# A mixture of experts in pairs: tokens gathered for two pairs at a time from two rounded parts, and the scatter-back moved into the next pair's first product

## The chip, the cores and the metric

The program runs on one core of a Trainium2 chip. Its five engines run side by side and meet at semaphores: TensorE (PE in the profile; PEld is its weight load), VectorE (DVE), ScalarE (ACT), GpSimd (POOL) and SyncE (SP), which issues most of the DMAs. The metric is device time in microseconds (us), and lower is better. The kernel before took 2449.71 us, the median of 3 runs (2448.79 to 2453.85).

## The reference

`first_block` has two layers on 512 tokens of 1024 channels. Each layer is a mixer (a recurrent one, then a convolutional one) and after it a mixture of 16 experts. `second_block` then runs two more hybrid layers. The change touches the mixture alone, so it is what matters here:

```python
def _ec_moe(h, router, w1, w3, w2):
    cap = EC_CAPACITY * n // N_EXPERTS                      # 2 * 512 / 16 = 64 tokens an expert
    probs = softmax(h @ router, over the experts)
    gates, idx = lax.top_k(probs, cap)                      # every expert takes its 64 best tokens
    xs = h[bidx, idx]                                       # gather
    a = xs @ w1[e];  g = xs @ w3[e]                         # 1024 x 1024 each
    y = (silu(a) * g) @ w2[e] * gates                       # 1024 x 1024
    return zeros_like(h).at[bidx, idx].add(y)               # scatter back
```

`h` is `x` divided by its root mean square and multiplied and shifted per channel (`G` and `SH` in the kernel). All inputs are float32. Each layer reads 16 * 3 matrices of 4 MB, so 192 MB (192 loads of 1 MB) a layer.

## The kernel before

One `Builder` writes the whole program. A scheduler then sets the order on each engine from the dependencies and from its own estimate of times, so the order of the code is not the order on the engine.

`moe(l, fin)` handles the 16 experts of layer `l` in 8 pairs (`q`). The 64 tokens of one expert of a pair stand in rows 0 to 63, and those of the other in rows 64 to 127. The work of a pair is:

- **Gather** (L1104, `pick` at L1113): a matrix `oh` with a single 1 in each column, 512 tokens by 128 slots, picks the tokens. For each of 8 groups of channels, 4 float32 products of 128 columns (L1116) sum the tokens of `xn` (`x` times `rr`, made at L1093) into a PSUM bank. DVE (even groups, L1120) or ACT (odd groups, L1118) applies `G` and `SH` and writes `xs`.
- **Products** (`expert_mm`, L1132): `xs` is the stationary operand, 64 columns of it per expert, so that the two experts use the two halves of the array. For each 2 loads of weights (one per expert) there are 8 products of 512 columns, 4 for each half. w1, w3 and w2 take 32 products each (L1141; for w2 of the last pair L1239).
- **Gates** (L1122): 4 float32 products of 2 columns give every slot its probability.
- **Between w3 and w2**: ACT computes silu (L1196), DVE multiplies (L1197), PE transposes in two PSUM banks (L1205), and two copies follow (L1206).
- **Scatter** (`weigh` L1207, `scatter` L1213): DVE multiplies the result by the gates (L1209), ACT rounds it to float32r (L1210) and DVE takes the rest (L1211). For 4 blocks of tokens and 2 halves of the channels, 2 float32r products of 512 columns (L1217) with the matrix `sc` go to a bank `ac`, which DVE adds to `x` (L1218). `sc` comes from two small products with `eid` (L1190).

A float32 product is two instructions in the trace, each with its own weight load. A float32r product is one.

PSUM has 8 banks: 4 are called `mm`, 2 `tr` and 2 `ac`. The weights go through a ring of 1 MB tiles: 4 of the general ring, 1 of the persistent pool and `EXTRA` = 13 of their own, 18 in all. `EORDER` says in which order the ring takes them. SP loads a tile as soon as PE has finished with the one that stood there 18 loads earlier (L318). The first 18 loads go ahead of the first product.

The gather of a pair is written after the pair before it has done w3, and the scheduler draws part of it forward into w2 and into the next w1. The first pair (its tokens come from `rk`, a rank computed while routing) is gathered between its first products. Meanwhile DVE ranks all the experts (`topk`, L1144) for the later pairs.

Of the kernel before, what the change touches and what calls it, by code (L numbers as in the profile page):

```python
# [25 lines left out]
NT = 4  # L26
# [243 lines left out]
class Builder:  # L270
    NBASE = 4
    X1, X2, X3, X4, X5, X6 = 2, 1, 3, 1, 7, 1
    NSTREAM, SDEPTH, SBUFS = 3, 2, 4
    EXTRA = 13
    EORDER = ((3, 2, 8, 9, 10, 7, 11, 0, 1, -1, -1, -1, -1, 4, 5, 6, -2, 12), (-1, 7, 0, 6, 1, 8, 9, 10, -1, -1, 5, 11, -1, 2, 3, 4, -2, 12))

    def __init__(self, ctx, tc, a, out):
        self.ctx, self.tc, self.nc, self.a, self.out = ctx, tc, tc.nc, a, out
# [800 lines left out]
    def moe(self, l, fin):  # L1079

        nc, a, tc, x = self.nc, self.a, self.tc, self.x
        G, SH, pr, rr = self.G, self.SH, self.pr, self.rr
        self.rw.close()
        es = ExitStack()
        mp = es.enter_context(tc.tile_pool(name=f"M{l}", bufs=1, side="right", reuse_waits="tile"))
        pos = mp.tile([16, 512], BF16, name=f"pos{l}")
        pT = mp.tile([P, NT, 16], F32, name=f"pT{l}")
        gts = mp.tile([P, 8], F32, name=f"gts{l}")
        xn = self.pp.tile([P, NT, D], F32, tag="hp0", name=f"xn{l}")
        rt = self.pp.tile([P, KD // 2, 512], F32, tag="hp1", name=f"rt{l}")  # L1090
# [13 lines left out]
        def gather(q):  # L1104

            oh = mp.tile([P, NT, 2, 64], F32, tag="oh", name=self.nm("oh"))
            ps = pT[:, :, 2 * q:2 * q + 2] if q else self.rk
            self.oh = nc.vector.tensor_tensor(oh, self.iota[:, None, None, :].to_broadcast([P, NT, 2, 64]),  # L1108
                                    ps[:, :, :, None].to_broadcast([P, NT, 2, 64]), op=ALU.is_equal)
            xs = mp.tile([P, KD, P], F32, tag="xsT", name=self.nm("xsT"))  # L1110
            return xs, oh

        def pick(k, xs, oh):  # L1113
            p = self.mm("tr")[:, :P]
            for t in range(NT):
                nc.tensor.matmul(p, xn[:, t, k * P:(k + 1) * P], oh[:, t].rearrange("p e s -> p (e s)"), start=(t == 0), stop=(t == NT - 1))  # L1116
            if k % 2:
                nc.scalar.activation(out=xs[:, k], in_=p, func=AF.Identity, scale=G[:, k:k + 1], bias=SH[:, k:k + 1])  # L1118
            else:
                nc.vector.tensor_scalar(xs[:, k], p, G[:, k:k + 1], SH[:, k:k + 1], op0=ALU.mult, op1=ALU.add)  # L1120
# [41 lines left out]
        nxt = gather(0)  # L1162
        oh0 = self.oh
# [4 lines left out]
        nc.scalar.activation(out=pe, in_=p[:16], func=AF.Copy)  # L1168
        for q in range(8):
            xs, oh = nxt  # L1170
            acc = []
            first = lambda i: (pick(2 * i, xs, oh), pick(2 * i + 1, xs, oh))
            for n in range(2):
                pa = [self.mm() for _ in range(2)]
                expert_mm(pa, lambda k, s: xs[:, k, 64 * s:64 * s + 64], first if q + n == 0 else None)
                acc.append(pa)
            gates(q, oh)

            p = self.mm("tr")
# [33 lines left out]
            def scatter(t, j, e):  # L1213
                js = slice(j * 512, (j + 1) * 512)
                p = self.mm("ac")
# [1200 lines left out]
```

## Time and profile before

| | |
|---|---|
| median of 3 runs | 2449.71 us |
| profiled execution | 2447.41 us, its span 2445.2 us |
| PE busy | 2291.8 us (94%) |
| DVE, ACT, POOL busy | 1018.9, 628.4, 361.7 us |
| mixture of layer 0, first gather to the last scatter | 441.5 to about 962 us |
| mixture of layer 1 | 1181.4 to about 1700 us |
| L1141, expert products | 2944 instructions |
| L1116, gather | 1024 instructions |
| L1217, scatter | 256 instructions |

The page cuts the span into 40 slices of 61 us. The mixtures are slices 8 to 15 and 20 to 27, where PE and the DMA engines both read 9 in nearly every slice. A busy PE is not PE at its peak, since ends are modelled and overlap. What a piece of work costs is therefore read from the start of one row to the start of the next.

### The profile page before, as it was taken

The page shows a single profiled execution, that of the slowest core. Times are in us where ns is not written, and L with a number is a line of the kernel's source. Part 1 is how long each engine was busy: PE and PEld are TensorE (multiplying, and loading weights), DVE is VectorE, ACT ScalarE, POOL GpSimd, SP SyncE. Part 2 cuts the span into 40 slices and gives each one's busy share as a digit, 9 for nine tenths or more (in the row PEclk, how much of TensorE's full clock was granted, in tenths as well). Part 3 has the DMA queues.
Part 4 walks back from the last instruction along what each step waited for, and adds up shares of the span by engine and source line. Part 5 has one row for each costly group of instructions (what it writes and reads, how often), then busy time and mean ns, then how long its engine had stood idle before and what let it go on. Part 6 is the DMA issues. An engine that isn't in the chain of part 4 may idle for free. (4 is left out here: it accounts for less than half of the span.)

```text
span 2445.2 us, 30723 instructions
## 1 busy us (share of the span) xinstructions
PE 2291.8 (94%) x12368; PEld 1380.9 (56%) x12368; DVE 1018.9 (42%) x2053; ACT 628.4 (26%) x1173; POOL 361.7 (15%) x390
## 2 busy tenths in 40 slices
PE   7996899999999998999999999997999889999998
PEld 2772487544444443666544444442766667777776
DVE  5545463412222213783422222213665665635642
ACT  3235123200000003333210000003443334423442
POOL 2221113000000001003000000001233441232232
PEclk9997799999999999998999999999999999999999
DMA  8537215889999994654789999996210221141131
GB/s 313 185 108 275 87 69 233 312 324 397 389 388 390 394 405 163 227 204 189 293 326 389 388 389 396 392 401 212 74 53 27 65 69 49 31 133 57 48 108 69
DMA packets 190199, 551.69 MB, mean 226 GB/s; under 512 B 12625, under 2 KB 69849, under 8 KB 182762
## 3 DMA queue, kind: packets, MB, share of 16 engines
q1 hardware_dynamic: 186282, 533.47, 57.3%
q0 software_dynamic: 2768, 11.71, 1.4%
q10 hardware_dynamic: 1008, 4.56, 0.5%
q8 instruction: 97, 1.59, 0.3%
q14 instruction: 44, 0.36, 0.0%
HBM read 545.51 MB, written 4.19 MB: 225 GB/s over the span
## 5 line engine op out<-in xcount | busy, mean ns | idle before, releaser
L1141 PE MATMUL mm<-ring,xsT 128*64 128x512 f32 x2048 | 502.4, 597 | 0.0
L1141 PEld LDWEIGHTS mm<-ring,xsT 128*64 128x64 f32 x2048 | 172.7, 137 | 268.8 <-issue 264.6
L1141 PE MATMUL ac<-ring,em 128*64 128x512 f32 x896 | 224.8, 597 | 0.0
L1497 PE MATMUL ac<-hC,sth 128*128 128x512 f32 x504 | 210.9, 419 | 2.8 <-ACT msg L2193 2.2
L1498 PE MATMUL ac<-hC,sth 128*128 128x512 f32 x504 | 205.7, 408 | 0.0
L1499 PE MATMUL ac<-hC,stl 128*128 128x512 f32 x504 | 203.3, 403 | 0.0
L1197 DVE TENSOR_TENSOR em<-em,mm 128x512 f32<-128x512 f32 x32 | 21.9, 688 | 360.7 <-PE mm L1141 360.7
L1116 PEld LDWEIGHTS tr<-oh,xn 128*128 128x128 f32 x1024 | 124.4, 198 | 69.0 <-issue 40.3
L1116 PE MATMUL tr<-oh,xn 128*128 128x128 f32 x1024 | 137.6, 288 | 18.2 <-DVE oh L1108 10.9
L1141 PEld LDWEIGHTS ac<-ring,em 128*64 128x64 f32 x896 | 69.9, 136 | 125.9 <-issue 120.9
L1473 ACT ACTIVATE sth<-ring 128x512 fp32r<-128x512 f32 x126 | 79.4, 632 | 144.8 <-PE ac L1498 127.2
L1497 PEld LDWEIGHTS ac<-hC,sth 128*128 128x128 f32 x504 | 96.0, 191 | 27.2 <-ACT msg L2193 4.5
L1218 DVE TENSOR_TENSOR x<-ac,x 128x512 f32<-128x512 f32 x128 | 84.1, 688 | 59.9 <-PE ac L1217 57.8
L1498 PEld LDWEIGHTS ac<-hC,sth 128*128 128x128 f32 x504 | 95.8, 190 | 19.9 <-issue 2.1
L1499 PEld LDWEIGHTS ac<-hC,stl 128*128 128x128 f32 x504 | 95.7, 190 | 20.1 <-issue 0.2
L334 POOL TENSOR_TENSOR wsl<-ring,wsh 128x1024 fp32r<-128x1024 f32 x7 | 16.7, 2387 | 592.1 <-ACT wsh L340 592.1
L1118 ACT ACTIVATE xsT<-tr,modc,gain 128x128 f32<-128x128 f32 x64 | 29.3, 458 | 275.7 <-PE mm L1141 157.6
L1217 PE MATMUL ac<-ey,sc 128*128 128x512 f32 x256 | 81.8, 429 | 17.9 <-DVE ey L1211 10.3
L1196 ACT ACTIVATE em<-mm 128x512 f32<-128x512 f32 x32 | 18.9, 598 | 304.7 <-PE mm L1141 304.7
L904 PE MATMUL mm<-pwh,cp 128*128 128x512 f32 x256 | 86.7, 418 | 4.7 <-ACT cp L1417 3.2
L334 DVE TENSOR_TENSOR stl<-ring,sth 128x512 fp32r<-128x512 f32 x84 | 63.3, 755 | 62.9 <-ACT sth L1473 61.1
L1217 PEld LDWEIGHTS ac<-ey,sc 128*128 128x128 f32 x256 | 41.5, 188 | 82.8 <-DVE x L1218 27.3
(781 smaller groups left out, 3698.6 us busy)
## 6 DMA issues: line engine op xcount, KB each, us to landing
ring<-in_exp_w_dram SPq DMA_DIRECT2D x384, 1024.0 KB, 9.1
ring<-in_w_in_dram SPq DMA_DIRECT2D x40, 1024.0 KB, 5.3
mblk<-in_w_mod_dram SPq DMA_DIRECT2D x40, 1024.0 KB, 5.0
ring<-in_cf_w_dram SPq DMA_DIRECT2D x12, 1024.0 KB, 7.5
ring<-in_w_out_dram SPq DMA_DIRECT2D x8, 1024.0 KB, 5.1
ring<-in_w_mod_dram SPq DMA_DIRECT2D x4, 1024.0 KB, 21.7
hW<-in_w_mod_dram SPq DMA_DIRECT2D x4, 1024.0 KB, 24.1
wbr<-in_w_branch_dram SPq DMA_DIRECT2D x16, 256.0 KB, 2.6
```

What stands on the lines that cost most here:

```text
L334: (self.nc.gpsimd if self.nlo % self.lomod == 0 else self.nc.vector).tensor_tensor(out, a, b, op=ALU.subtract)
L904: nc.tensor.matmul(ps[t], u, v[:, k], start=(bias is None and s == 0 and k == 0 and i == 0), stop=(s == 3 and k == 1 and i == 2))
L1116: nc.tensor.matmul(p, xn[:, t, k * P:(k + 1) * P], oh[:, t].rearrange("p e s -> p (e s)"), start=(t == 0), stop=(t == NT - 1))
L1118: nc.scalar.activation(out=xs[:, k], in_=p, func=AF.Identity, scale=G[:, k:k + 1], bias=SH[:, k:k + 1])
L1141: nc.tensor.matmul(ps[j][64 * s:64 * s + 64, :], lhs(k, s), wt[s][:, kk, j * 512:(j + 1) * 512], start=(k == 0), stop=(k == KD - 1))
L1197: nc.vector.tensor_tensor(m[:, js], m[:, js], acc[1][j], op=ALU.mult)
L1217: nc.tensor.matmul(p, sc[:, t * P:(t + 1) * P], e[:, i], start=(i == 0), stop=(i == 1))
L1218: nc.vector.tensor_tensor(x[:, t, js], p, x[:, t, js], op=ALU.add)
L1473: nc.scalar.activation(out=hi, in_=src, func=AF.Copy)
L1497: nc.tensor.matmul(self.sps, hi[:, k], hh, start=(kk == 0), stop=False)
L1498: nc.tensor.matmul(self.sps, hi[:, k], hl, start=False, stop=False)
L1499: nc.tensor.matmul(self.sps, lo[:, k], hh, start=False, stop=(kk == KD - 1))
```

## The change

Five things change in `moe`; nothing outside it does.

1. **Gather for two pairs.** The groups are pair 0, pair 1, then (2, 3), (4, 5), (6, 7). `x * rr` is kept as a float32r part `xnh` (ACT) and its rest `xnl` (DVE). For each group of channels, 8 float32r products (4 blocks of tokens by 2 parts) of 256 columns (128 for pair 1) go to half a PSUM bank. The 8 groups of channels fill four banks, `tr` and `ac` in turn.
2. **The first pair** is gathered from `x` itself, with `rr` in place of the 1 (`oh0`).
3. **Scatter later.** The scatter of a pair is called ahead of blocks 2 and 3 of the next pair's w1, and its odd token blocks use `tr` banks.
4. **Gates** are made with the gather, as products of 4 float32r columns (two parts of two probabilities) that DVE sums.
5. **Ring.** The new tiles take room: `EXTRA` is 10, so the ring has 15 tiles instead of 18.

```diff
-    EXTRA = 13
-    EORDER = ((3, 2, 8, 9, 10, 7, 11, 0, 1, -1, -1, -1, -1, 4, 5, 6, -2, 12), (-1, 7, 0, 6, 1, 8, 9, 10, -1, -1, 5, 11, -1, 2, 3, 4, -2, 12))
+    EXTRA = 10
+    EORDER = ((3, 2, 8, 9, 7, 0, 1, -1, -1, -1, -1, 4, 5, 6, -2), (-1, 7, 0, 6, 1, 8, 9, -1, -1, 5, -1, 2, 3, 4, -2))
...
-        with tc.issue_after(self.last_exp.ins):
-            for t in range(NT):
-                nc.scalar.activation(out=xn[:, t], in_=x[:, t], func=AF.Copy, scale=rr[:, t:t + 1])
...
+        def pick(qs, xs, oh):
+            w = len(qs) * P
+            for k0 in range(0, KD, 2):
+                p = self.mm("ac" if k0 % 4 else "tr")
+                for k in (k0, k0 + 1):
+                    pk = p[:, (k - k0) * 256:(k - k0) * 256 + w]
+                    for i in range(2):
+                        for t in range(NT):
+                            nc.tensor.matmul(pk, xn[i][:, t, k * P:(k + 1) * P], oh[:, t, 0:len(qs)].rearrange("p q s -> p (q s)"),
+                                             start=(i == t == 0), stop=(i == 1 and t == NT - 1))
+                for k in (k0, k0 + 1):
+                    modulate(k, xs[:, k, 0:len(qs)].rearrange("p q s -> p (q s)"), p[:, (k - k0) * 256:(k - k0) * 256 + w])
...
+                        nc.tensor.matmul(p[:, 4 * i:4 * i + 4], oh[:, t, i], prp[:, t, q].rearrange("p u e -> p (u e)"),
+                                         start=(t == 0), stop=(t == NT - 1))
...
+        for t in range(NT):
+            for e in range(2):
+                nc.vector.tensor_scalar(oh0[:, 0, t, 64 * e:64 * e + 64], self.iota, self.rk[:, t, e:e + 1], rr[:, t:t + 1],
+                                        op0=ALU.is_equal, op1=ALU.mult)
...
+        def rest(i):
+            if left and i in (2, 3):
+                for t in (0, 1) if i == 2 else (2, 3):
+                    for j in range(2):
+                        left[0](t, j)
...
+                for t in range(NT):
+                    nc.scalar.activation(out=xn[0][:, t], in_=x[:, t], func=AF.Copy, scale=rr[:, t:t + 1])
+                    nc.vector.scalar_tensor_tensor(xn[1][:, t], x[:, t], rr[:, t:t + 1], xn[0][:, t].bitcast(F32), op0=ALU.mult, op1=ALU.subtract)
...
-            if q < 7:
-                nxt = gather(q + 1)
-                for k in range(KD):
-                    pick(k, *nxt)
+            if q == groups[g][-1] and q < 7:
+                xs, oh = gather(groups[g + 1])
+                pick(groups[g + 1], xs, oh)
+                gates(groups[g + 1], oh)
...
-                p = self.mm("ac")
+                p = self.mm("tr" if q < 7 and t % 2 else "ac")
...
-                for t in range(NT):
-                    for j in range(2):
-                        scatter(t, j, ey[:, j])
+                left.append(lambda t, j, f=scatter, ey=ey: f(t, j, ey[:, j]))
```

What the scheduler makes of it shows in the order on the engines. On PE, before, this is where w2 of a pair (`ac`) ends, its scatter (L1217) runs and w1 of the next pair (`mm`) begins:

```order
L1141 MATMUL ac_3558<-ring_652_3597,em_3489 64x512
L1141 MATMUL mm_3646<-ring_664_3648,xsT_3496 64x512
L1217 MATMUL ac_3614<-ey_3607,sc_3485 128x512 x2
L1217 MATMUL ac_3618<-ey_3607,sc_3485 128x512 x2
L1141 MATMUL mm_3647<-ring_664_3648,xsT_3496 64x512
L1217 MATMUL ac_3622<-ey_3607,sc_3485 128x512 x2
L1217 MATMUL ac_3626<-ey_3607,sc_3485 128x512 x2
L1141 MATMUL mm_3646<-ring_665_3650,xsT_3496 64x512
L1141 MATMUL mm_3647<-ring_665_3650,xsT_3496 64x512
L1141 MATMUL mm_3646<-ring_664_3648,xsT_3496 64x512
L1217 MATMUL ac_3630<-ey_3607,sc_3485 128x512 x2
L1217 MATMUL ac_3634<-ey_3607,sc_3485 128x512 x2
```

And this is the same place with the change:

```order
L1268 MATMUL tr_3670<-ey_3629,sc_3558 128x512
L1166 MATMUL mm_3636<-ring_638_3638,xsT_3268 64x512
L1166 MATMUL mm_3637<-ring_638_3638,xsT_3268 64x512
L1268 MATMUL ac_3662<-ey_3629,sc_3558 128x512 x2
L1268 MATMUL ac_3666<-ey_3629,sc_3558 128x512 x2
L1268 MATMUL tr_3670<-ey_3629,sc_3558 128x512
L1268 MATMUL tr_3674<-ey_3629,sc_3558 128x512 x2
L1166 MATMUL mm_3636<-ring_639_3640,xsT_3268 64x512
L1166 MATMUL mm_3637<-ring_639_3640,xsT_3268 64x512
L1166 MATMUL mm_3636<-ring_638_3638,xsT_3268 64x512
L1166 MATMUL mm_3636<-ring_639_3640,xsT_3268 64x512
```

The scatter now stands in three groups instead of four, each with more banks, but its first product is the first thing behind w2, with no other product between. The two products that follow read one ring tile, so both are of one expert.

The second place is w1 of a pair, where the rest of the gather that was drawn forward lies. On PE, before (`tr_3772` is a bank of the gather):

```order
L1217 MATMUL ac_3642<-ey_3607,sc_3485 128x512 x2
L1141 MATMUL mm_3647<-ring_665_3650,xsT_3496 64x512
L1141 MATMUL mm_3646<-ring_666_3660,xsT_3496 64x512
L1141 MATMUL mm_3647<-ring_666_3660,xsT_3496 64x512
L1116 MATMUL tr_3772<-oh_3763,xn_2690 128x128 x3
L1141 MATMUL mm_3646<-ring_667_3662,xsT_3496 64x512
L1141 MATMUL mm_3647<-ring_667_3662,xsT_3496 64x512
L1141 MATMUL mm_3646<-ring_666_3660,xsT_3496 64x512
L1141 MATMUL mm_3646<-ring_667_3662,xsT_3496 64x512
L1141 MATMUL mm_3647<-ring_666_3660,xsT_3496 64x512
L1141 MATMUL mm_3647<-ring_667_3662,xsT_3496 64x512
L1116 MATMUL tr_3772<-oh_3763,xn_2690 128x128
```

And with the change, in pair 3, which gathers for pairs 4 and 5:

```order
L1127 MATMUL ac_3800<-oh_3778,xnl_2691 128x256
L1166 MATMUL mm_3636<-ring_641_3652,xsT_3268 64x512
L1166 MATMUL mm_3637<-ring_641_3652,xsT_3268 64x512
L1166 MATMUL mm_3636<-ring_640_3650,xsT_3268 64x512
L1166 MATMUL mm_3636<-ring_641_3652,xsT_3268 64x512
L1166 MATMUL mm_3637<-ring_640_3650,xsT_3268 64x512
L1166 MATMUL mm_3637<-ring_641_3652,xsT_3268 64x512
L1127 MATMUL tr_3781<-oh_3778,xnh_2690 128x256 x4
L1127 MATMUL tr_3781<-oh_3778,xnl_2691 128x256 x4
L1127 MATMUL tr_3781<-oh_3778,xnh_2690 128x256 x4
L1166 MATMUL mm_3636<-ring_646_3678,xsT_3268 64x512
L1166 MATMUL mm_3637<-ring_646_3678,xsT_3268 64x512
```

Before, 8 of a pair's 32 gather products lay in w2 and w1, and the other 24 came right behind w3. Now the 64 products for two pairs lie in seven pieces in w1 of pairs 1, 3 and 5 (the last piece, of one product, behind the first two of w3), and w1 is cut into runs of 6 and 2 products between them. Behind w3 follow only the gates (L1146) and the transposes (L1256). The other pairs have no gather: behind the scatter stand 54 products of w1 and w3 in one run. Pair 1 itself is gathered for the most part right behind w3 of pair 0.

At the start of the mixture the order on DVE, before, after the rank `rk` is known:

```order
L1070 SCALAR_TENSOR_TENSOR rk_2153<-rk_2153,tr_2644 128x8
L1108 TENSOR_TENSOR oh_2774<-iota,rk_2153 128x512
L1149 MAX m_513_2921<-rt_2691 16x8
L990 MEMSET rk_5991 128x2
L1150 MATCH_REPLACE rt_2691<-m_513_2921,rt_2691 16x512
L1120 TENSOR_SCALAR xsT_2776<-tr_2785,gain_2132,modc 128x128
```

And with the change:

```order
L1070 SCALAR_TENSOR_TENSOR rk_2153<-rk_2153,tr_2644 128x8
L1234 SCALAR_TENSOR_TENSOR xnl_2691<-x,rrm_2156,xnh_2690 128x1024
L1190 TENSOR_SCALAR oh_2757<-iota,rk_2153,rrm_2156 128x64 x8
L1192 TENSOR_TENSOR oh_2757<-iota,rk_2153 128x512
L1117 TENSOR_SCALAR xsT_2767<-tr_2776,gain_2132,modc 128x128
L1174 MAX m_511_2914<-rt_2693 16x8
L1234 SCALAR_TENSOR_TENSOR xnl_2691<-x,rrm_2156,xnh_2690 128x1024
L1175 MATCH_REPLACE rt_2693<-m_511_2914,rt_2693 16x512
L1234 SCALAR_TENSOR_TENSOR xnl_2691<-x,rrm_2156,xnh_2690 128x1024
L1174 MAX m_512_2917<-rt_2693 16x8
L1234 SCALAR_TENSOR_TENSOR xnl_2691<-x,rrm_2156,xnh_2690 128x1024
L1117 TENSOR_SCALAR xsT_2767<-tr_2796,gain_2132,modc 128x128
```

One of the four `xnl` operations of 1024 columns now stands between the rank and the matrix that the first gather waits for, and three more stand between the first two writes of `xs`.

## Rows read from the trace of the kernel before

**Rows 1.** Busy time by stretch: us, PE, PEld, DVE, ACT, POOL, clock, DMA share, GB/s.
```profile
600.00:640.00 40.00, 38.45 (x204) 19.16 (x201) 3.94 (x9) 4.18 (x8) 0.00 (x0) 1.00 1.02 418
640.00:680.00 40.00, 39.25 (x162) 15.57 (x162) 8.73 (x13) 2.39 (x4) 0.00 (x0) 1.00 0.94 373
```
**Rows 2.** Waits of SP's DMA queue, 380 to 1000 us: total, times, longest.
```profile
SPq L318 <- PE mm L1141: 249.2, 76, 16.8
SPq L318 <- PE ac L1141: 155.7, 36, 10.1
```
**Rows 3.** PE by time, one pair: start us, us, work, [idle before].
```profile
561.24 8.80 PE L1141 MATMUL ac<-ring,em 128*64 128x512 f32 x36
...
583.68 1.07 PE L1141 MATMUL mm<-ring,xsT 128*64 128x512 f32 x2
584.68 1.20 PE L1217 MATMUL ac<-ey,sc 128*128 128x512 f32 x4
585.82 1.93 PE L1141 MATMUL mm<-ring,xsT 128*64 128x512 f32 x6
...
597.67 20.87 PE L1141 MATMUL mm<-ring,xsT 128*64 128x512 f32 x96
619.09 5.62 PE L1116 MATMUL tr<-oh,xn 128*128 128x128 f32 x48 [0.55 <-ACT xsT L1118]
624.55 1.37 PE L1205 MATMUL tr<-ident,em 128*128 128x128 f32 x8
625.85 4.51 PE L1141 MATMUL ac<-ring,em 128*64 128x512 f32 x20
```
**Rows 4.** PE by time: first w2 and, without a gather, the last pair, layer 0.
```profile
496.59 8.80 PE L1141 MATMUL ac<-ring,em 128*64 128x512 f32 x36
...
884.41 8.80 PE L1141 MATMUL ac<-ring,em 128*64 128x512 f32 x36
...
903.11 1.43 PE L1217 MATMUL ac<-ey,sc 128*128 128x512 f32 x4 [1.57 <-DVE ey L1211]
...
936.85 0.66 PE L1205 MATMUL tr<-ident,em 128*128 128x128 f32 x4
...
938.29 7.94 PE L1239 MATMUL mm<-ring,em 128*64 128x512 f32 x34
```
**Rows 5.** PE by time, layer 1: first w2 and last w2.
```profile
1236.13 12.23 PE L1141 MATMUL ac<-ring,em 128*64 128x512 f32 x52
...
1675.57 7.94 PE L1239 MATMUL mm<-ring,em 128*64 128x512 f32 x34
```
**Rows 6.** PE by time, two neighbouring float32r products of 512 columns.
```profile
1763.67 0.40 PE L1498 MATMUL ac<-hC,sth 128*128 128x512 f32 x1
1763.90 0.40 PE L1499 MATMUL ac<-hC,stl 128*128 128x512 f32 x1
```
**Rows 7.** DVE and ACT groups: busy us, mean ns | idle before (last: whole span).
```profile
L1120 DVE TENSOR_SCALAR xsT<-tr,gain,modc 128x128 f32<-128x128 f32 x32 | 13.1, 408 | 28.3 <-PE tr L1116 28.3
...
L1197 DVE TENSOR_TENSOR em<-em,mm 128x512 f32<-128x512 f32 x16 | 11.0, 689 | 185.2 <-PE mm L1141 185.2
...
L1206 ACT COPY em<-tr 128x512 f32<-128x512 f32 x16 | 9.4, 587 | 15.3 <-PE tr L1205 15.3
...
L334 DVE TENSOR_TENSOR wsl<-ring,wsh 128x1024 fp32r<-128x1024 f32 x29 | 37.7, 1302 | 38.5 <-ACT wsh L340 38.5
```
**Rows 8.** PE by time, the first gather and product of layer 0.
```profile
441.52 3.53 PE L1116 MATMUL tr<-oh,xn 128*128 128x128 f32 x16
444.98 3.65 PE L1141 MATMUL mm<-ring,xsT 128*64 128x512 f32 x16
```
**Rows 9.** Busy time by stretch, as in rows 1, layer 1 and the last pair.
```profile
1225.00:1226.00 1.00, 0.02 (x1) 0.05 (x1) 0.80 (x2) 0.98 (x2) 0.00 (x0) 1.00 1.08 442
...
1226.00:1230.00 4.00, 4.00 (x21) 4.00 (x22) 1.60 (x3) 2.27 (x4) 0.00 (x0) 0.57 1.01 417
...
940.00:960.00 20.00, 17.29 (x69) 5.74 (x66) 6.37 (x11) 7.10 (x18) 0.06 (x1) 1.00 0.22 66
```

More of the change, by code (lines that the diff above doesn't have):

```diff
@@ L1102, in moe @@
         slot = self.col("slot")
[L1104 to L1110, printed above, removed]
-            return xs, oh
@@ L1113, in pick, with gather @@
-        def pick(k, xs, oh):
+        def gather(qs):
+            n = len(qs)
+            oh = mp.tile([P, NT, 2, P], F32R, tag="oh", name=self.nm("oh"))
+            o = oh[:, :, 0:n].rearrange("p t q (e s) -> p t (q e) s", e=2)
+            nc.vector.tensor_tensor(o, self.iota[:, None, None, :].to_broadcast([P, NT, 2 * n, 64]),
+                                    pT[:, :, 2 * qs[0]:2 * qs[0] + 2 * n, None].to_broadcast([P, NT, 2 * n, 64]), op=ALU.is_equal)
+            xs = mp.tile([P, KD, 2, P], F32, tag="xsT", name=self.nm("xsT"))
+            return xs, oh
@@ L1114, in pick, with pick_first @@
+        def pick_first(k):
             p = self.mm("tr")[:, :P]
             for t in range(NT):
[L1116 to L1120, printed above, removed]
@@ L1160, in topk @@
             nc.gpsimd.tensor_copy(pos, cs)
-        nxt = gather(0)
-        oh0 = self.oh
+        oh0 = mp.tile([P, 2, NT, P], F32, tag="oh", name=self.nm("oh"))
+        for t in range(NT):
+            for e in range(2):
+                nc.vector.tensor_scalar(oh0[:, 0, t, 64 * e:64 * e + 64], self.iota, self.rk[:, t, e:e + 1], rr[:, t:t + 1],
+                                        op0=ALU.is_equal, op1=ALU.mult)
+        ohi = nc.vector.tensor_tensor(oh0[:, 1].rearrange("p t (e s) -> p t e s", e=2), self.iota[:, None, None, :].to_broadcast([P, NT, 2, 64]),
+                                      self.rk[:, :, :, None].to_broadcast([P, NT, 2, 64]), op=ALU.is_equal)
+        xs = mp.tile([P, KD, 2, P], F32, tag="xsT", name=self.nm("xsT"))
         pe, cs, on = (rt[:16, i] for i in range(3))
@@ L1168, in moe @@
         nc.scalar.activation(out=pe, in_=p[:16], func=AF.Copy)
+        left, groups = [], ((0,), (1,), (2, 3), (4, 5), (6, 7))
+        def rest(i):
[3 more added lines that the diff above has]
+                        left[0](t, j)
+                if i == 3:
+                    left.clear()
         for q in range(8):
-            xs, oh = nxt
+            g = q if q < 2 else q // 2 + 1
+            qi = q - groups[g][0]
             acc = []
-            first = lambda i: (pick(2 * i, xs, oh), pick(2 * i + 1, xs, oh))
+            first = lambda i: (pick_first(2 * i), pick_first(2 * i + 1))
             for n in range(2):
                 pa = [self.mm() for _ in range(2)]
-                expert_mm(pa, lambda k, s: xs[:, k, 64 * s:64 * s + 64], first if q + n == 0 else None)
+                expert_mm(pa, lambda k, s: xs[:, k, qi, 64 * s:64 * s + 64], first if q + n == 0 else rest)
                 acc.append(pa)
-            gates(q, oh)
+            if q == 0:
+                gates((0,), None)
             p = self.mm("tr")
@@ L1182, in moe @@
                 for t in range(NT):
-                    nc.tensor.transpose(p[:, t * P:(t + 1) * P], oh[:, t].rearrange("p e s -> p (e s)"), self.ident)
+                    nc.tensor.transpose(p[:, t * P:(t + 1) * P], oh0[:, 1, t], self.ident)
                 nc.scalar.activation(out=sc, in_=p, func=AF.Copy)
                 g2 = self.bcast_gate(mp, l, 1)
-                with tc.issue_after(oh0.ins):
+                with tc.issue_after(ohi.ins):
                     topk()
+                for t in range(NT):
+                    nc.scalar.activation(out=xn[0][:, t], in_=x[:, t], func=AF.Copy, scale=rr[:, t:t + 1])
+                    nc.vector.scalar_tensor_tensor(xn[1][:, t], x[:, t], rr[:, t:t + 1], xn[0][:, t].bitcast(F32), op0=ALU.mult, op1=ALU.subtract)
+                for t in range(NT):
+                    v = pr[:, t].rearrange("p (q e) -> p q e", e=2)
+                    nc.scalar.activation(out=prp[:, t, :, 0], in_=v, func=AF.Copy)
+                    nc.vector.tensor_tensor(prp[:, t, :, 1], v, prp[:, t, :, 0].bitcast(F32), op=ALU.subtract)
             else:
@@ L1211, in weigh, with scatter @@
                 nc.vector.tensor_tensor(e[:, 1], p, e[:, 0].bitcast(F32), op=ALU.subtract)
[L1213 removed]
+            def scatter(t, j, e, sc=sc, q=q):
                 js = slice(j * 512, (j + 1) * 512)
[L1215 removed]
+                p = self.mm("tr" if q < 7 and t % 2 else "ac")
                 for i in range(2):
@@ L1225, in moe @@
                     weigh(py[j], j, ey[:, j])
-                for t in range(NT):
-                    for j in range(2):
-                        scatter(t, j, ey[:, j])
+                left.append(lambda t, j, f=scatter, ey=ey: f(t, j, ey[:, j]))
                 continue
-            ey = [mp.tile([P, 2, 512], F32R, tag="xsT", name=self.nm("ey"))]
+            ey = [mp.tile([P, 2 * KD * P], F32R, tag="xsT", name=self.nm("ey"))[:, 0:1024].rearrange("p (i n) -> p i n", i=2)]
             for j in range(2):
```

24 lines of the change are left out of this document (19 added, 5 removed).

## The prediction, made before the change was run

> **What bounds the kernel now.** I read the table of stretches first, then SP's waits, then PE by time. In the mixture the clock is full, PE is busy nearly all the time and the DMA engines too, so either could be the bound [rows 1]. SP's queue tells which: the loads stand and wait until PE has finished with a tile, 405 us in all over the first mixture [rows 2], and no wait of PE for a ring tile was to be found there. So PE sets the pace, and DMA is close behind it. One pair takes 625.85 - 561.24 = 64.61 us [rows 3], and six pairs in each layer take that.
>
> Inside a pair I read starts. A run of expert products costs by the fuller half of the array: 18 products of which 10 fall on one half show 8.80 us, three with 2 on one half 1.93, a single one 1.07 [rows 3], so 0.858 us per product on the fuller half and 0.22 of tail. The next work starts 1.00 us after the start of the single one, so a run costs 0.858 h + 0.14. The run of 48 (24 a half) gives 20.8 by this and shows 20.87. A group of 4 scatter products takes 585.82 - 584.68 = 1.14 us [rows 3]. Float32r products of 512 columns start 0.23 us apart [rows 6], so 4 of them are 0.92, and a switch into full-width work costs 0.22. Of the gather, 48 instructions take 624.55 - 619.09 = 5.46 us, 0.114 each, so a pair's 64 cost 7.3 us.
>
> **The change, part by part.** *Pairs without a gather* (2, 4, 6 and 7). The trace has such a pair already, the last one: 938.29 - 884.41 = 53.88 us [rows 4]. With the change the 8 gate instructions go; at the 0.114 of the gather's they are 0.9 us, with the switch 1.0 to 1.1. The scatter's first product stands alone behind w2: PE waits for the rounded part `ey`. The old pair waited 1.57 us for the rest of it, one DVE operation later [rows 4]; I take 1.1 for the new one, between 0.9 and 1.6. Runs of 2 (both of one expert), 6 and 2 count h = 2, 4, 2, and 54 counts 28. Summed, this is 13.9 (w2, h = 16) + 1.1 + 4.6 (16 scatter products, four switches) + 7.3 + 24.1 + 1.5 (behind w3, 936.85 to 938.29) = 52.5 and the two small products of `eid`, which both have. By the trace's pair, 53.9 - 1.0, it is 52.9 us, which I take.
>
> *Pairs with a gather for two* (1, 3, 5). To the 52.9 come 64 products of 256 columns. No float32r product under 512 columns is in the trace. The bounds are 0.114 (the float32 instruction of 128 columns) and 0.232 (float32r of 512). I take half the columns of the latter and its overhead, 0.107 + 0.019 = 0.126: 8.1 us. The seven pieces cost seven switches, 1.5. Instead of one run of 54 (h = 28, 24.1 us) PE does runs of 6, 2, 6, 2, 6, 2 and 30, h = 4, 2, 4, 2, 4, 2, 16, together 34: 29.2 + 7 times 0.14 = 30.2, so 6.1 more. Behind w3 nothing is left to fill: DVE multiplies twice (0.69 each), then writes four of the eight `xs` groups. A write of 128 columns is 0.41 [rows 7], of 256 about 0.52. The `tr` banks that gates and transposes want come free only with these writes. The gates start 1.6 us behind w3, the first transposes at 2.75, the second when the gates' bank is read (3.4), and w2 after the first copy (0.59) at 4.2, against 1.5 without a gather [rows 4]: 2.7 more. Sum: 52.9 + 8.1 + 1.5 + 6.1 + 2.7 = 71.3 us.
>
> Two pairs take 52.9 + 71.3 = 124.2 instead of 129.2 us. In layer 0, from the first w2 to that of the last pair, before 938.29 - 496.59 = 441.7 us [rows 4], it is 3 x 71.3 + 4 x 52.9 = 425.5: 16.2 less. In layer 1, 1675.57 - 1236.13 = 439.4 [rows 5]; there pair 1 has w2 and 16 products of w1 in one run (h = 54 in all instead of 58, and no wait for `ey`), so 66.3: 66.3 + 142.6 + 211.6 = 420.5, 18.9 less. Together 35.1 us.
>
> *The start of each layer.* Now one `xnl` operation stands ahead of `oh0` on DVE: 1.30 us by the subtraction of 1024 columns [rows 7]. Three more (3.9 us) and two steps of `topk` lie between the first two writes of `xs`, against 3.65 us of products on PE [rows 8] and the next gather; I take two waits of PE of 0.7. Then there are eight small operations for `oh0` instead of one (0.2, since PE can begin with the first), and the gates of pair 1 now stand ahead of w2 (0.5). Sum 3.4 a layer, 6.8 in all, between 2 and 12 (the clock is low at this point: 16 instructions take 3.5 us [rows 8] where 0.114 each would be 1.8, and a longer wait can keep it low).
>
> Pair 1's gather has products of 128 columns: 64 by 0.114, as now, at the least, since each has a weight load as the float32 ones have; 64 by 0.232 at the most, 7.5 us more a layer. I take the lower end, which is the row with the same columns, and keep the upper for the range.
>
> *The clock.* Behind w3 PE now has 4.2 us with little in it, six times. In layer 1 PE stood idle for one such microsecond, after small products, and the next four ran at 0.57 [rows 9], so at 1.2 GHz for most of it: 0.43 x 4 = 1.7 us lost. At the last pair, with waits of 1.5 us between dense runs, the clock stayed at 1.00 [rows 9]. I count half: 6 x 0.85 = 5.1 us, between 0 and 10.
>
> *The feed.* A pair needs 25.17 MB. A pair of 52.9 us asks for 476 GB/s, one of 71.3 for 353, two together for 405. With a full queue DMA brings 418 [rows 1]. In a short pair 25.17 - 0.418 x 52.9 = 3.1 MB are missing, three tiles of the 15, and the next long pair gives them back; the two short ones at the end take six. So the smaller ring costs nothing as long as 418 holds. The DMA page of the Trainium skill (DMA: Bandwidth & Descriptors, Specifications) gives about 358 GB/s as what HBM grants a core. That speaks against the change, since a pair would then take 70.3 us; the trace's 418 over 40 us goes past it, and the row decides.
>
> Sum: -35.1 + 6.8 + 5.1 = -23.2 us. The profiled execution took 2447.41, so 2424.2; the median of the runs lies 2.3 above that execution: 2426.5 us.
>
> **The rivals.** (a) *The feed holds at the average of before*, 25.17 MB in 64.6 us = 390 GB/s, with bursts cut short by 15 tiles. For: the second stretch shows 373 at a share of 0.94 [rows 1]. Against: there SP was waiting for PE, and where it wasn't, 418 came. Then two pairs take 129.2 us again, and the start and the clock remain: +11.9, 2462 us, slower than before. It decides from 405 GB/s down.
>
> (b) *A float32r product of 256 columns costs what one of 512 does*, 0.232: six gathers x 64 x 0.106 = 40.7 more, 2467 us. For: no narrower one was ever timed here. Against: nothing in the trace; float32 products get cheaper with columns. The gain is gone from 0.186 us on.
>
> (c) *PE keeps strict order*, so that two products of one expert hold up the other half. The Trainium skill says that matmuls start and end in program order (TensorE: Matmul & The Clock Gate, Part 3, The mechanism). Then each block in the order "two of one, two of the other" would take half as long again, 6.9 us for a w2 of 32, about 2500 us. But before, the run of 48 stands in just this order and ran at full rate [rows 3].
>
> (d) *The gaps are smaller than I think*: the clock holds, and the banks come free sooner. 2426.5 - 5.1 - 6 x 1.5 - 4 = 2408 us or less.
>
> **How the numbers follow.** Forecast 0.74, with its own range of 2409 to 2442 (the clock's 5 either way, 15 for pair 1's gather, 5 for the start, 12 for the gap and the gather's 0.114); (a) 0.09, (b) 0.09, (c) 0.02, (d) 0.06. The range of 2404 to 2450 leaves out most of (a) to (c). No change means within 0.2%, which is about what a measurement of this kernel can tell: 2444.8 to 2454.6. Faster is the forecast and (d) and a small part of the rest, 0.81; same 0.07 (a milder feed limit); slower 0.12.
>
> **What would show it.** Right: starts of w2 alternate by about 53 and 71 us; float32r products of 256 columns start 0.12 to 0.13 us apart; PE waits 4 us in all behind w3 of pairs 1, 3 and 5, on `xsT` writes; no wait of PE for a ring tile. The first product of each layer starts 1.5 us later than before. Wrong: PE waiting for the ring, gather products 0.2 us apart, or pairs of equal length. If the clock drops in every gap, the rows behind w3 read 0.5 to 0.6.

## The result, and the profile after

The changed kernel takes 2423.4 us (median of 4 runs, 2416.4 to 2435.3), the kernel before 2449.9: ratio 0.9889, 95% interval 0.9859 to 0.9918. The forecast was 2426.5. The profiled execution has a span of 2419.0 us, 26.2 less than before; the forecast for it was 23.2 less.

PE by time, the third gather for two and what follows it in layer 0 (answers to [rows 3, 4]; columns as there):

```profile
747.19 14.00 PE L1166 MATMUL ac<-ring,em 128*64 128x512 f32 x64
761.92 0.49 PE L1268 MATMUL tr<-ey,sc 128*128 128x512 f32 x1 [0.73 <-ACT ey L1261]
...
774.81 3.65 PE L1166 MATMUL mm<-ring,xsT 128*64 128x512 f32 x12
778.39 0.74 PE L1127 MATMUL tr<-oh,xnh 128*128 128x256 f32 x4
778.97 0.64 PE L1127 MATMUL tr<-oh,xnl 128*128 128x256 f32 x4
779.45 0.64 PE L1127 MATMUL tr<-oh,xnh 128*128 128x256 f32 x4
780.01 1.93 PE L1166 MATMUL mm<-ring,xsT 128*64 128x512 f32 x4
781.87 0.74 PE L1127 MATMUL tr<-oh,xnl 128*128 128x256 f32 x4
...
799.26 13.95 PE L1166 MATMUL mm<-ring,xsT 128*64 128x512 f32 x60
815.17 1.05 PE L1146 MATMUL tr<-prp,oh 128*128 128x4 f32 x8 [1.96 <-ACT xsT L1115]
816.09 1.28 PE L1256 MATMUL tr<-ident,em 128*128 128x128 f32 x8
817.42 14.00 PE L1166 MATMUL ac<-ring,em 128*64 128x512 f32 x64
...
870.02 14.00 PE L1166 MATMUL ac<-ring,em 128*64 128x512 f32 x64
...
922.58 7.94 PE L1288 MATMUL mm<-ring,em 128*64 128x512 f32 x34
```

Starts of w2 alternate as forecast: 817.42 - 747.19 = 70.2 us with a gather for two (forecast 71.3), 870.02 - 817.42 = 52.6 without (52.9). Four float32r products of 256 columns take 779.45 - 778.97 = 0.48, 0.12 each (0.126). Of the runs between the pieces of the gather, one of 6 products takes 778.39 - 774.81 = 3.58 and one of 2 takes 781.87 - 780.01 = 1.86. The gates wait 1.96 us behind w3 for a write of `xsT`. No product of PE waits for a ring tile; weight loads do, six times in the two mixtures, 1.5 us in all and 0.4 at the longest. SP's queue still waits for PE (answers to [rows 2], 380 to 1000 us):

```profile
SPq L318 <- PE mm L1166: 272.8, 105, 20.2
SPq L318 <- PE ac L1166: 89.5, 27, 10.8
```

By place, with the stretches cut at the last product of `route_warm`, the first w2 and the last pair of each layer, the 26.2 us are:

| stretch, us | before | after | difference | forecast |
|---|---|---|---|---|
| up to layer 0's mixture | 440.31 | 441.46 | +1.2 | 0 |
| start of layer 0 | 56.28 | 58.38 | +2.1 | +3.4 |
| pairs of layer 0 | 441.70 | 422.74 | -19.0 | -16.2, and 2.6 of clock |
| between the layers | 241.91 | 244.72 | +2.8 | 0 |
| start of layer 1 | 55.93 | 61.15 | +5.2 | +3.4 |
| pairs of layer 1 | 439.44 | 417.25 | -22.2 | -18.9, and 2.6 of clock |
| the rest | 769.63 | 773.30 | +3.7 | 0 |

At layer 0's start DVE writes one part of `xn` ahead of the one-hot rows (rows of DVE by time; before, the comparison stood directly behind `rk`):

```profile
441.71 1.28 DVE L1234 SCALAR_TENSOR_TENSOR xnl<-x,rrm,xnh 128x1024 fp32r<-128x1024 f32 x1
442.91 1.87 DVE L1190 TENSOR_SCALAR oh<-iota,rk,rrm 128x64 f32<-128x64 f32 x8
```

In layer 1 the gather for pair 1 runs at half clock behind a wait (PE by time; rows between left out):

```profile
1212.97 0.63 PE L1127 MATMUL tr<-oh,xnh 128*128 128x128 f32 x4 [1.13 <-DVE oh L1108]
...
1214.65 1.05 PE L1127 MATMUL tr<-oh,xnl 128*128 128x128 f32 x4
1215.50 1.05 PE L1127 MATMUL ac<-oh,xnh 128*128 128x128 f32 x4
...
1228.45 15.22 PE L1166 MATMUL ac<-ring,em 128*64 128x512 f32 x64
```

0.85 for four is 0.21 each; in layer 0, where no wait stood ahead, they take 0.11. The wait alone doesn't explain this. In e6 below it is as long, but eight products of w3 lie among the small operations ahead of it (before the change it was six), and the gather and w2 run at full clock (e6, PE by time):

```profile
1191.65 3.65 PE L1166 MATMUL mm<-ring,xsT 128*64 128x512 f32 x12
...
1196.78 0.63 PE L1127 MATMUL tr<-oh,xnh 128*128 128x128 f32 x4 [1.14 <-DVE oh L1108]
...
1205.80 13.95 PE L1166 MATMUL ac<-ring,em 128*64 128x512 f32 x64 [0.16 <-DVE em L1259]
```

Layer 1's start takes 57.5 us there instead of 61.15. That is one execution, and no run was made for this question, so the cause of the fall there stays open. The clock behind the gaps of pairs 1 and 5 of layer 0 (columns as in [rows 1]; the eighth figure is the granted clock):

```profile
568.70:573.00 4.30, 4.26 (x13) 1.31 (x14) 0.51 (x1) 0.61 (x2) 0.00 (x0) 0.60 1.03 422
...
817.40:822.00 4.60, 4.58 (x22) 1.78 (x24) 0.69 (x1) 0.00 (x0) 0.00 (x0) 1.00 1.02 415
```

At 0.60, so at 1.2 GHz for most of it, that w2 takes 15.70 instead of 14.00 us. It happens in two of the six gaps.

### The profile page after: what moved, and what is told of

It is laid out like the page before. It is cut to its first block, busy times and chain, and to the rows that moved or that the text cites. A ratio compares the mean times of both kernels' runs of the same rounds, so it can differ in the third digit from the quotient of the medians.

```text
span 2419.0 us, 29841 instructions
## 1 busy us (share of the span) xinstructions
PE 2271.6 (94%) x11928; PEld 1361.9 (56%) x11928; DVE 1020.4 (42%) x2047; ACT 615.7 (25%) x1153; POOL 361.0 (15%) x390
## 4 chain that ended last, share of the span: by engine, by line
PE 71%; DVE 5%; POOL 3%; ACT 2%; issue 1%; DMA 1%; POOLq 0%; DVEq 0%; ACTq 0%; SPq 0%
PE mm L1166 22%; PE ac L1166 8%; PE ac L1546 4%; PE mm L904 4%; PE ac L1547 4%; PE ac L1548 4%; PE mm L351 3%; PE mm L1655 2%; PE ac L1268 2%; PE ac L1127 2%; PE tr L1127 2%; PE ac L351 2%; PE tr L1268 1%; PE mm L1288 1%; PE tr L1703 1%
## 5 line engine op out<-in xcount | busy, mean ns | idle before, releaser
L1166 PE MATMUL mm<-ring,xsT 128*64 128x512 f32 x2048 | 542.6, 598 | 0.3
L1166 PEld LDWEIGHTS mm<-ring,xsT 128*64 128x64 f32 x2048 | 182.9, 136 | 294.1 <-issue 284.0
L1166 PE MATMUL ac<-ring,em 128*64 128x512 f32 x896 | 199.4, 603 | 0.4 <-DVE em L1257 0.2
L1166 PEld LDWEIGHTS ac<-ring,em 128*64 128x64 f32 x896 | 76.5, 139 | 114.0 <-issue 109.6
L1546 PEld LDWEIGHTS ac<-hC,sth 128*128 128x128 f32 x504 | 97.1, 193 | 26.2 <-ACT msg L2242 4.3
L1247 ACT ACTIVATE em<-mm 128x512 f32<-128x512 f32 x32 | 18.9, 597 | 347.5 <-PE mm L1166 347.4
L1260 DVE SCALAR_TENSOR_TENSOR ac<-ac,gts,gate 128x512 f32<-128x512 f32 x28 | 21.2, 759 | 189.1 <-PE ac L1166 187.7
L351 PE MATMUL mm<-hB,wsh 128*128 128x512 f32 x256 | 85.2, 407 | 1.4 <-ACT hB L418 0.7
L1269 DVE TENSOR_TENSOR x<-ac,x 128x512 f32<-128x512 f32 x72 | 47.0, 687 | 77.4 <-PE ac L1268 77.3
L334 POOL TENSOR_TENSOR stl<-ring,sth 128x512 fp32r<-128x512 f32 x42 | 54.4, 1295 | 155.1 <-ACT sth L1522 154.8
L351 PE MATMUL ac<-hA,wsh 128*128 128x512 f32 x224 | 71.4, 399 | 0.0
## 6 DMA issues: line engine op xcount, KB each, us to landing
ring<-in_exp_w_dram SPq DMA_DIRECT2D x384, 1024.0 KB, 10.9
```

Of the source, the lines that this page charges most:

```text
L334: (self.nc.gpsimd if self.nlo % self.lomod == 0 else self.nc.vector).tensor_tensor(out, a, b, op=ALU.subtract)
L351: self.nc.tensor.matmul(p[:, :n], x[:, k], y[:, k], start=(k == 0 and i == 0), stop=(stop and k == K - 1 and i == 2))
L1546: nc.tensor.matmul(self.sps, hi[:, k], hh, start=(kk == 0), stop=False)
```

## The experiments

All start from the changed kernel except e7; ratios are to the kernel before.

**e1, the gather behind w3.**

```
+ lastw3 = self.lastmm                 # last product of w3
+ with tc.issue_after(lastw3.ins):
      pick(groups[g + 1], xs, oh)
```

> The gather's products are held until the last product of w3, nothing else is changed; w1 and w3 of pairs 1, 3 and 5 then run unsplit. My theory (a run costs by its fuller half, so the pieces 6, 2, 6, 2, 6, 2 and 30 cost 6 us more than one of 54, and seven switches 1.5 more; and the gap behind w3 is there only because the gather stood ahead of it): on PE alone such a pair falls from 70.2 to about 60.5 us, 52.6 + 64 x 0.118 + 0.2, since the multiplications and the writes of xsT now lie beside the gather. Pairs 2, 4, 6, 7 stay at 52.6. Two pairs then ask for 50.3 MB in 113 us, 445 GB/s, more than the 418 to 420 that the loads get with a full queue, so the feed must show for the first time: PE waits for ring tiles late in each layer, some 5 to 11 us a layer in my bookkeeping of 15 tiles. Sum per layer about -26 + 8, so 2380 to 2392 us, with granted clock 1.00 behind w3. Rival 1 (the pieces cost nothing, since PE would stand behind w3 anyway for the same writes): 2415 to 2430. Rival 2 (the feed gives more than 420 when asked): no wait for the ring, 2368 to 2374.

2377.0 us, ratio 0.9701 (0.9677 to 0.9725). PE by time in layer 0:

```profile
606.22 14.00 PE L1166 MATMUL ac<-ring,em 128*64 128x512 f32 x64
...
633.08 24.25 PE L1166 MATMUL mm<-ring,xsT 128*64 128x512 f32 x108
657.26 0.74 PE L1127 MATMUL tr<-oh,xnh 128*128 128x256 f32 x4
...
664.94 0.95 PE L1146 MATMUL tr<-prp,oh 128*128 128x4 f32 x8
...
667.19 14.00 PE L1166 MATMUL ac<-ring,em 128*64 128x512 f32 x64 [0.15 <-DVE em L1259]
```

The pair falls from 70.2 to 667.19 - 606.22 = 61.0 us; the 64 products behind w3 are done in 7.7, the gates no longer wait, and w2 behind all six gathers for two reads 14.0. At the layer's end products of PE wait for the ring, as none did before, while DMA brings 418 GB/s (PE by time, then a stretch as in [rows 1]):

```profile
846.18 3.65 PE L1166 MATMUL ac<-ring,em 128*64 128x512 f32 x12 [0.52 <-DMA ring<-in_exp_w_dram]
...
896.54 3.85 PE L1290 MATMUL mm<-ring,em 128*64 128x512 f32 x16 [0.82 <-DMA ring<-in_exp_w_dram]
```

```profile
840.00:890.00 50.00, 47.66 (x183) 18.19 (x180) 9.34 (x15) 2.39 (x4) 0.00 (x0) 1.00 1.03 418
```

Both steps of the theory hold; the median lies 3 us under its range.

**e2, a gather for each pair.**

```
- groups = ((0,), (1,), (2, 3), (4, 5), (6, 7))
+ groups = tuple((i,) for i in range(8))
```

> Exact parts, four banks and the late scatter stay, but every gather serves one pair (64 products of 128 columns for each of the pairs 1 to 7) instead of two. My theory: the gain of the change is the pairing. A float32r product of 128 columns costs 0.112, nearly what one of 256 does (0.118), so each pair pays 7.2 us of products, and the pieces of 6 and 2 with their switches (some 12 us), and a gap behind w3: pairs 1 to 6 take 70 to 75 us instead of 70.2 and 52.6 by turns, 60 to 75 us more a layer, 2540 to 2575 in all, slower than the kernel before. Rival (the gain is the late scatter and the four banks, and the gather's width matters little): pairs of 61 to 62 us, 2420 to 2435.

2566.8 us, ratio 1.0473 (1.0451 to 1.0496). A pair takes 646.60 - 571.24 = 75.4 us:

```profile
571.24 15.70 PE L1166 MATMUL ac<-ring,em 128*64 128x512 f32 x64 [0.24 <-ACT em L1257]
...
644.57 0.61 PE L1146 MATMUL tr<-prp,oh 128*128 128x4 f32 x4 [1.72 <-ACT xsT L1115]
...
646.60 3.62 PE L1166 MATMUL ac<-ring,em 128*64 128x512 f32 x8 [0.24 <-ACT em L1257]
```

So with the gather where the change puts it, the change without the pairing is slower than the old kernel. The width of the gather is not all that this run changes. It also cuts w1 and w3 in every pair: ten runs of 6 and 2 by turns and one of 14 count h = 38 where one of 54 counts 28, which by the rule of the prediction is 10.0 us, with 2.2 for ten switches, more than the 7.2 of the products. And the gates wait in 11 places, and behind all 11 the clock reads 0.57 to 0.66 over the next 4 us (w2 15.4 to 15.7); behind the one gather without such a wait it reads 1.00. An estimate for a gather per pair behind w3, from e1's rows: 52.6 + 7.2 + 0.7 (61.0 less 52.6 and 7.7) is 60.5 us, under the 64.6 of the old kernel. No run tests this, so how much of the gain needs the pairing stays open.

**e3, the scatter back behind w2.**

```
- left.append(lambda t, j, f=scatter, ey=ey: f(t, j, ey[:, j]))
+ for t in range(NT):
+     for j in range(2):
+         scatter(t, j, ey[:, j])
```

> Only the scatter goes back: it is issued right behind w2's weighting instead of inside the third and fourth block of the next w1; gather for two, four banks and gates stay. My theory: PE waits for the second parts of ey and for DVE's additions, 0.7 to 1.5 us more in each of the 13 pairs after the first, and there are fewer pieces (-0.5): pairs of 53 to 54 and 70.5 to 71.5, 2423 to 2440. Rival (the scatter's place is where the change gains): pairs come back to 58 and 75, 2480 or more.

2403.5 us, ratio 0.9806 (0.9784 to 0.9827): neither theory. It is 20 us faster than the changed kernel. PE by time, between w2 and the long run of a pair without a gather:

```profile
874.12 0.50 PE L1268 MATMUL tr<-ey,sc 128*128 128x512 f32 x1 [0.73 <-ACT ey L1261]
874.56 1.07 PE L1166 MATMUL mm<-ring,xsT 128*64 128x512 f32 x2
875.56 1.21 PE L1268 MATMUL ac<-ey,sc 128*128 128x512 f32 x4
876.61 0.85 PE L1268 MATMUL tr<-ey,sc 128*128 128x512 f32 x3
877.29 1.12 PE L1268 MATMUL ac<-ey,sc 128*128 128x512 f32 x4
878.35 1.08 PE L1166 MATMUL mm<-ring,xsT 128*64 128x512 f32 x4
879.36 1.19 PE L1268 MATMUL tr<-ey,sc 128*128 128x512 f32 x4
880.48 3.65 PE L1166 MATMUL mm<-ring,xsT 128*64 128x512 f32 x14
...
884.39 24.25 PE L1166 MATMUL mm<-ring,xsT 128*64 128x512 f32 x108
```

The waits that I expected don't come: one stands there, the 0.73 that the late scatter has too. And the ten products of w1 among the scatter's are cut into 1, 2 and 7, with 1 + 1 + 4 on the fuller half, where the changed kernel has 2, 6 and 2 with 2 + 4 + 2. Two fewer at 0.858 are 1.7; the pair is 52.6 - (910.08 - 859.38 = 50.7) = 1.9 shorter. My rule gave this, had I applied it.

**e4, the start freed.**

```
  for t in range(NT): nc.scalar.activation(out=xn[0][:, t], ...)
+ with tc.issue_after(ohi.ins):
      for t in range(NT): nc.vector.scalar_tensor_tensor(xn[1][:, t], ...)
```

> Only the start of a layer: the four operations for the second part of xn on DVE are held behind the last of the one-hot rows; nothing else is changed. My theory: the one of them that stands ahead of the rows (1.28 us) holds up the first gather, so the first product of each layer comes 1.3 us earlier than in the changed kernel (5.7 instead of 7.1 us after the last comparison on DVE), and the whole 2 to 3 us faster: 2418 to 2422, which the spread of the runs may hide. Rival (the half clock at this point sets the time, not DVE): the first product moves, but the products that follow run at half clock for longer and the second run of products starts when it did.

2417.0 us, ratio 0.9868 (0.9844 to 0.9892), within the spread. From the start of the last `route_warm` products to the first gather it is 1.06 us instead of 2.13, in both layers. Layer 0's start is 1.6 us shorter, layer 1's 0.4: there the half clock at pair 1's gather remains (w2 15.45). The first product moved, as the theory says; the end moved in one layer only. In the kernels that keep the changed kernel's start, layer 0's takes 54.9 to 58.5 us (e6, e3), so of the 1.6 only the 1.07 of the first product is sure.

**e5, e1 with e3 and e4** (the three diffs above in one kernel).

> The three edits of e1, e3 and e4 together: gather behind w3, scatter right behind w2's weighting, start of a layer freed. On PE alone the early scatter takes 1.87 us off each of the pairs after the first (11.0 instead of 12.9 us from w2's end to the long run), some 12 a layer, and the start 1.3 a layer. My theory (the feed of 418 to 420 GB/s, one tile per 2.5 us, is now the bound): the feed gives back nearly all of the 12: PE waits for ring tiles from pair 5 on, 15 to 18 us a layer instead of the 8.7 in e1, so a layer is 3 us shorter by the scatter and 1.3 by the start: 2366 to 2371 us. Rival (PE is the bound, and e1's waits for the ring come from the end of a layer alone): the gains add up, 2348 to 2353.

2378.8 us, ratio 0.9708 (0.9687 to 0.9729): not told apart from e1. The feed gave back all, not three quarters: the pairs of a layer take 396.5 and 397.2 us, in e1 397.5 and 397.1. Waits for the ring in both layers (total us, times, longest), of PE's products and weight loads:

```profile
PEld mm L1166 <- DMA ring<-in_exp_w_dram: 26.4, 27, 1.5
PE mm L1166 <- DMA ring<-in_exp_w_dram: 8.8, 16, 0.6
PEld ac L1166 <- DMA ring<-in_exp_w_dram: 7.4, 8, 1.5
```

In e1 the products of these lines wait six times, 3.1 us, and their weight loads 12.1; here it is 20 times and 10.9 us (with four of `ac`, 2.1), and 33.8. The median above my range is not the mixture's: the rest after layer 1 took 782.9 us against 775.8 in e1, in code that both share.

**e6, e1 with 12 ring tiles.**

```
- EORDER = ((3, 2, 8, 9, 7, 0, 1, -1, ...), (-1, 7, 0, 6, 1, 8, 9, -1, ...))
+ EORDER = ((3, 2, 7, 0, 1, -1, ...), (-1, 7, 0, 1, -1, ...))     # 8, 9 and 6 go
```

> e1 with 12 ring tiles instead of 15 in each layer, nothing else. My theory (DMA works without a pause once the ring has free tiles, so a layer ends when 192 tiles have come, and each tile less in the ring at the start is 2.5 us later at the end): 7.5 us a layer, 15 in all, 2390 to 2394 us, PE waiting for the ring from pair 4 on. Rival 1 (the waits in e1 come from something at the end of a layer): 2375 to 2380. Rival 2 (12 tiles are too few to keep the loads in flight, and the rate itself falls under 410 GB/s): 2400 or more.

2394.5 us, ratio 0.9769 (0.9744 to 0.9793), 17.5 more than e1 where 15 were expected. The pairs take 405.3 and 404.7 us, 7.7 more a layer: three tiles of 2.5 us. The rest of the difference lies outside the pairs (the rest after layer 1 takes 784.0 us).

**e7, the kernel before with the ring of 15.**

```
- EXTRA = 13
- EORDER = ((3, 2, 8, 9, 10, 7, 11, ...), ...)     # 18 tiles a layer
+ EXTRA = 10
+ EORDER = ((3, 2, 8, 9, 7, 0, 1, ...), ...)       # 15, as in the changed kernel
```

> The kernel before with the changed kernel's ring of 15 tiles (instead of 18), nothing else. My theory: its pairs of 64.6 us ask for 390 GB/s, under the 418 that DMA brings, so the ring is always full before PE comes and three tiles more or less cost nothing: within 0.2% of the kernel before, 64.6 us a pair, no wait for the ring. Rival (the smaller ring was a price that the change paid): pairs of 65 us and more, 2460 or more.

2449.5 us, ratio 1.0004 (0.9992 to 1.0015); a pair takes 64.6 us, and weight loads wait for the ring 1.7 us in all, in seven short waits. The last two pairs of layer 0 take 66.3 and 55.4 in the profiled run: behind waits of 0.88 and 1.58 us, which the kernel before has too, the clock falls (0.89 in 814.5 to 830 us, 0.81 in 896 to 905). So such falls are not the change's alone.

**e8, the gap behind w3 filled.**

```
+ if len(groups[g + 1]) == 2:
+     wp = self.mm()
+     with tc.issue_after(lastw3.ins):
+         for _ in range(15):
+             nc.tensor.transpose(wp[:, 0:P], self.ident, self.ident)
  gates(groups[g + 1], oh)
```

> The changed kernel with 15 transposes of the identity (their result is not used) on PE in the gap behind w3 of pairs 1, 3 and 5, where it otherwise waits 1.96 us for a write of xsT. My theory (the clock falls behind some of these gaps, because PE stands still between dense work and the small gate products; in the traces so far in 2 to 4 of the 6, at 0.6 to 2.6 us each with the transposes of em that follow): the gates start when they did, the clock reads 1.00 behind all six, every w2 there takes 14.0 us; 2 to 6 us faster than the changed kernel, 2417 to 2422. Rival (the fall comes from elsewhere, the small gate products or a cause outside the core): w2 behind some of the gaps still reads 14.5 to 15.8, 2421 to 2427.

2415.8 us, ratio 0.9866 (0.9842 to 0.9889), just under my range. PE by time behind w3 of pair 1, where the changed kernel had 15.70 (here the row is cut after 48):

```profile
560.43 1.86 PE L1257 MATMUL mm<-ident 128*128 128x128 f32 x15
562.46 1.05 PE L1146 MATMUL tr<-prp,oh 128*128 128x4 f32 x8 [0.17 <-ACT xsT L1115]
563.38 1.28 PE L1262 MATMUL tr<-ident,em 128*128 128x128 f32 x8
564.71 10.57 PE L1166 MATMUL ac<-ring,em 128*64 128x512 f32 x48
```

w2 behind all six gaps reads 14.0, and the pairs take 419.6 and 416.6 us, 3.8 less in all than in the changed kernel. The intervals of the two ratios overlap; the rows tell what the medians can't.

**e9, e1 and e4, with ten transposes in layer 1's wait.**

```
+ if q == 0 and l:
+     wp = self.mm()
+     with tc.issue_after(self.lastT.ins):       # topk's last transpose
+         for _ in range(10):
+             lastw3 = nc.tensor.transpose(wp[:, 0:P], self.ident, self.ident)
```

> e1 (gather behind w3) and e4 (start freed), and in layer 1 ten transposes of the identity (result not used) on PE in the wait of 1.1 us for pair 1's one-hot rows, in front of pair 1's gather. My theory (that wait is where the clock falls in layer 1: the gather's products behind it ran at 0.21 instead of 0.11 and w2 took 15.2 to 15.7): the gather reads 0.11 a product, w2 14.0, 5 to 8 us less in front of layer 1's second pair, and 1.3 a layer at the start. What is saved there stays saved though the feed is the bound further on, since tiles come free sooner: 2367 to 2373 us. Rival (the feed's bound counts from an earlier point, so that PE only waits longer for the ring at the end): 2375 to 2380, the waits for the ring some 5 us longer in layer 1 than in e1.

2380.9 us, ratio 0.9728 (0.9705 to 0.9751): the theory was not put to the test, since the transposes came too late. Their bank had to be read by ACT first:

```profile
1187.25 2.39 PE L1257 MATMUL mm<-ident 128*128 128x128 f32 x10 [2.19 <-ACT em L1250]
1189.29 1.09 PE L1127 MATMUL tr<-oh,xnh 128*128 128x128 f32 x4
...
1205.70 15.81 PE L1166 MATMUL ac<-ring,em 128*64 128x512 f32 x64
```

PE stood still for 2.19 us instead of 1.13, and the products behind ran at half clock as before.

## Why the prediction was right

*What bounds the kernel.* PE, with DMA close behind: right on both sides. In the changed kernel no product waits for the ring; in e1, where two pairs ask for 50.3 MB in 113.5 us (443 GB/s), some do, and e5 and e6 show that the 12 us a layer that the scatter's place would save on PE then no longer show, and that a ring tile is worth 2.5 us a layer. The changed kernel, with two pairs in 122.8 us, asks for 410 and stays below this, so rival (a) fell: DMA brings 415 to 420 for long stretches and not 390. By the 358 GB/s of the Trainium skill (DMA: Bandwidth & Descriptors, Specifications) the bytes of a pair would need 70.3 us. The row there divides a stack's 716 GB/s by two cores, and this program runs on one; the 418 of e1 is the figure for this case.

*Pairs without a gather.* 52.6 for 52.9: the wait for `ey` is 0.73, where I took 1.1. The scatter stands in four groups, of 1, 7, 6 and 2 products (from 761.92, 764.21, 769.59 and 773.04 us), and not in the three that the section on the change names; the sum has the four switches.

*Pairs with a gather for two.* 70.2 for 71.3. The product of 256 columns costs 0.118, where I took 0.126 (rival (b) needed 0.186), and the gap behind w3 is as forecast (first product of w2 4.2 us behind w3's last). That the pieces cost 6.1 and not nothing stands in the rows: three runs of 3.58, three of 1.86 and 13.9 for the last 30 products are 30.2, as in the sum, against 24.2 for a run of 54. And e1 bears out the whole: without pieces, switches and gap the pair is 9.3 shorter, where 6.1 + 1.5 + 2.7 less the switch that stays is 10.1.

*The order on PE.* Rival (c) fell: a w2 of 32 products takes 14.0 us, 0.858 x 16 and a tail. Its price was too high, though. Only half of a block stands in the order "two of one, two of the other": with A and B for the two experts, a block of eight goes A A B B A B A B (the pieces of 2 and 6 in the listing of w1 are such a block cut in two), in the run of 48 too. The Trainium skill has matmuls start and end in program order (TensorE: Matmul & The Clock Gate, Part 3, The mechanism). By an estimate from the rows, with two instructions of 0.429 us to a product, such a block would then take 10 steps instead of 8, a quarter more and not half; for a w2 of four such blocks, as at 747.19 and 870.02, that is 3.4 us more. The 14.00 us of both leave no room for it.

*The start of a layer.* 2.1 and 5.2 for 3.4 each: 7.3 for 6.8 in all came out by luck, since the steps are not right. The first product comes 0.9 later than before (2.13 us behind the start of the last `route_warm` products instead of 1.21), where I had 1.5. The two later waits for `xs`, 1.4 in my sum, came to 0.1 in layer 1; in layer 0 the products there ran 1.0 slower, without a wait. In layer 1 three quarters are the half clock at pair 1's gather, 12.8 us for its 64 products (8.9 for as many instructions before); e6 shows that it need not be so. I had kept a price of 0.232 for them as an upper end, but as the price of the product; at full clock it is 0.112.

*The clock in the gap.* I took 5.1 for six gaps; in the profiled run it is 3.0 (pairs 2, 3 and 4 of layer 0, by 1.7, 0.8 and 0.5 over their like). With e3 and e4, 8 of 18 such gaps show it; e8, with the gap filled, 0 of 6, and e1, which has none, 0 of 6; in e2 it is all 11. So the mechanism is shown; in which gap of the changed kernel it strikes stays open.

*What was not in the sum.* The pairs gained 41.2 where 35.1 less 5.1 were forecast; stretches that the change doesn't touch gave back 7.6. So the 3 us between forecast and result are the difference of larger errors: the pairs were forecast 11 us too slow, and the 7.6 were not forecast. In the profiles of the eleven kernels, which share the code there, the rest behind layer 1 takes 769.6 to 784.0 us, with the clock in one and the same stretch of it, 500 to 600 us behind the last pair's start, at 0.91 in e3, e5, e6 and e8 (778.9 and more) and at 1.00 in the others (776.0 and less). The two kernels without the change have 769.6 and 771.4, but e2, which has most of it, has 771.1; whether the change has a hand in it is open.

*What the change left.* The forecast did not ask whether its pieces had to be. Behind w3, the gather gives 46 us more (e1); the scatter's new place costs 20 (e3), which the feed hides once the gather is moved (e5).

## What to carry to other kernels

Where two half arrays run side by side, count each run by its fuller half before other work is put into it: the place of a cut decides what it costs. When PE's work is shortened, divide the bytes by the time: beyond the rate of the loads the next saving is worth nothing, and only ring tiles or bytes are. A wait between dense work and small products can cost more behind it than in it, though not always (8 of 18 such gaps here); fill it with work whose bank is already free, or remove it.

## What was not expected of the hardware

Float32r products with full weights start 0.232 us apart at 512 columns [rows 6], 0.118 at 256 and 0.112 at 128: halving the columns once halves the time, halving them again gives nothing. The last of these, in layer 0, four each:

```profile
493.07 0.61 PE L1127 MATMUL ac<-oh,xnl 128*128 128x128 f32 x4
493.52 0.61 PE L1127 MATMUL ac<-oh,xnh 128*128 128x128 f32 x4
```

And DMA held 415 to 420 GB/s in e1, by stretches of 100 us, through the pairs of both layers (500 to 890 and 1250 to 1590 us), with 17.0 us from issue to landing (10.9 in the changed kernel), and 414 to 420 with 12 ring tiles: the loads lost nothing by the smaller ring, only their head start.
